# A U weights' cast placed behind a GELU, and gate one-hots built four tokens at a time, in a two-layer hybrid backbone

## The chip, the cores and the metric

The kernel runs on one core of a Trainium2 chip, in one launch. The metric is the time of an execution on the device in microseconds. Engines are named as in the profile: PE (TensorE, matmuls), PEld (its weight loads), DVE (VectorE), ACT (ScalarE), POOL (GpSimd) and SP (SyncE, which here only issues DMA transfers).

## The reference

Two layers work on 512 latent tokens and 256 context tokens of width 1024 in float32. In each layer a modulated norm feeds a token mixer (grouped-query attention and an RWKV-7 scan in two directions), and then a modulated norm feeds a layer of product-key experts (PEER):

```python
def peer_ffn(h, w_query, subkeys1, subkeys2, expert_u, expert_v):
    q = (h @ w_query).reshape(B, L, PEER_HEADS, 2, PEER_HALF)
    s1 = jnp.einsum('blhd,kd->blhk', q[..., 0, :], subkeys1)
    s2 = jnp.einsum('blhd,kd->blhk', q[..., 1, :], subkeys2)
    ...  # top 16 of each, top 16 of their sums: expert_idx; gates = softmax(top_score)
    u = jnp.take(expert_u, i_blk, axis=0)
    act = gelu(einsum('td,ted->te', h_blk, u))           # exact GELU
    v = jnp.take(expert_v, i_blk, axis=0)
    out = einsum('te,ted->td', g_blk * act, v)
```

There are 8 heads with 16 experts each for every token, out of 128 x 128 = 16384 experts. An expert's number is i1 * 128 + i2. The second layer needs no expert output for the context tokens.

## The kernel before

**Dense and gathered tokens.** Most token blocks (128 tokens each) go through *all* experts as dense products; the sparse choice enters as a weight that is zero for the experts that a token did not choose. In the first layer (`l == 0`) all four latent blocks are dense (`nd = 4`, 512 tokens, `TD = 512`) and the two context blocks are gathered, expert by expert, with indirect DMAs of GpSimd and multiply-adds of VectorE. In the second layer three latent blocks are dense and one is gathered. Gather steps are spread over the other work: `gafter(ins)` puts the next few of them behind an instruction `ins` of VectorE.

**A U product** (`ustep`) is the product of 128 experts' U rows (one value of i1) with all dense tokens, followed by the GELU. The weights come by a 512 KB DMA into a `raw` buffer. ScalarE casts them to `uhi` (`A.copy`, L1470), VectorE makes the remainder `ulo = ut - uhi` (L1471), and TensorE makes 24 matmuls (`mm3`, L158: 8 slices of the contraction, and for each high x high, high x low, low x high; the third is the first that reads `ulo`) into the PSUM tile `u_ps`. ScalarE's GELU (L1476) reads `u_ps` and writes `ga`. There are two `uhi` and two `ulo` buffers. The `raw` buffers (three in the first layer) are shared with the V weights (`vraw`).

**The gates' stretch.** For every dense block the chosen experts' i1, i2 and gates are transposed into `T3` (tile `gT`). `gstep` handles four tokens: it builds a one-hot of i2 times the gate (`o2`) and a one-hot of i1 (`o1`), both [128 choices, 128 places] for each token, and TensorE multiplies them (L1558) into `g_ps`: the 128 x 128 map of a token's gates. ScalarE copies it to `Gs` (L1560), from where it goes to DRAM (`gscr`). `o2` is made by four VectorE instructions, one a token (L1555: compare `iota` with i2, multiply by the gate). `o1` is made for odd groups by one VectorE comparison over four tokens (L1547), and for even groups by ScalarE: four Abs of `iota - i1` (L1552) and one Relu of one minus that (L1553). Each one-hot has three buffers. The first layer has 128 such steps, the second 96. Merged with them run U products whose `ga` is spilled to DRAM (`ustep(True)`): 43 in the first layer.

**The output stretch.** For each i1, `load_v` fetches and splits 128 V rows (`vhi` by ScalarE, `vlo` by VectorE), `load_u` fetches the spilled `ga` (as `gal`) or makes a new U product three steps ahead (`ustep(False)`, 85 in the first layer), and `weigh` multiplies `ga` by the gates `Gt` (a load of 1024 KB for every four i1) and splits the result into `whi` (ScalarE) and `wlo` (VectorE). `piece` then adds the products `whi`/`wlo` x `vhi`/`vlo` of two i1 (first layer) to the output: six of the eight pieces of the first layer gather in PSUM (`pa`), two go through one extra bank `po` and are added to SBUF by VectorE (L1637). PSUM is full in the first layer in this stretch: `u_ps` has *one* bank there (`ups[1] = 1`), and two in the second layer and in the gates' stretch.

**What sets the order.** The program names engine, operation and tiles. A planner (the Tile framework) turns it into one queue for each engine: it goes by the order of the program as priority, a model of each instruction's duration, and which buffer is free when. Each engine then works through its queue in that order and waits, at each instruction, for what that one needs. `merge` interleaves lists of steps in the program's order. `tc.issue_after(ins)` adds one more condition: the instructions in its block stand behind `ins` in the queue of its engine.

Of the kernel before, what the change touches and what calls it, by code (L numbers as in the profile page):

```python
# [10 lines left out]
F32 = mybir.dt.float32  # L11
# [5 lines left out]
AF = mybir.ActivationFunctionType  # L17
ALU = mybir.AluOpType
# [83 lines left out]
def body(ctx: ExitStack, tc: tile.TileContext, I: dict, out: bass.AP):  # L102
    nc = tc.nc
    V, A, G, PE, SP = nc.vector, nc.scalar, nc.gpsimd, nc.tensor, nc.sync
    mul, add, sub = ALU.mult, ALU.add, ALU.subtract
# [7 lines left out]
    def K(name):  # L113
        o, n = COFF[name]
        return cst[:, o:o + n]
# [38 lines left out]
    def mm3(ps, pairs, first, last):  # L154
        n = len(pairs)
        for q, (whi, wlo, hhi, hlo) in enumerate(pairs):
            for j, (a, b) in enumerate(((whi, hhi), (whi, hlo), (wlo, hhi))):
                PE.matmul(ps, a, b, start=first and q == 0 and j == 0, stop=last and q == n - 1 and j == 2)  # L158
# [1170 lines left out]
    def tail(L, cat, last, ro, need_ctx):  # L1329
        l = L["l"]  # L1330
# [40 lines left out]
        def gafter(ins, f=1.0):  # L1371
            pace[0] += pace[1] * f
            n = int(pace[0])
            pace[0] -= n
            if n and gq:
                with tc.issue_after(ins.ins):
                    gnext(n)
# [13 lines left out]
        op = eo.enter_context(tc.tile_pool(name=f"op{l}", bufs=1, side="right"))  # L1391
# [59 lines left out]
        pe = es.enter_context(tc.tile_pool(name=f"pe{l}", bufs=1))  # L1451
        gscr = dp.tile([NTC, 128, 128, GTC], F32, name=f"gscr{l}")
        gas = {}
        ucnt = [0]

        def raw():
            return pe.tile([128, KD, 128], F32, name="raw", bufs=RWB[l])
# [1 line left out]
        def wtiles():  # L1459
            return (raw(), pe.tile([128, KD, 128], F32R, name="uhi", bufs=2),  # L1460
                    pe.tile([128, KD, 128], F32R, name="ulo", bufs=2))

        def ustep(spill):
            i1 = ucnt[0]
            if i1 >= 128:
                return
            ucnt[0] += 1
            ut, uhi, ulo = wtiles()
            SP.dma_start(ut, I[f"ut{l}"][i1].rearrange("p (k c) -> p k c", c=128))
            A.copy(uhi, ut)  # L1470
            ins = V.tensor_tensor(ulo, ut, uhi.bitcast(F32), op=sub)  # L1471
            gafter(ins)
            ps = ups[0].tile([128, TD], F32, name="u_ps", bufs=ups[1])
            mm3(ps, [(uhi[:, k, :], ulo[:, k, :], hhi[:, k, :TD], hlo[:, k, :TD]) for k in range(KD)], True, True)
            ga = pe.tile([128, TD], F32, name="ga", bufs=5)
            A.activation(ga, ps, AF.Gelu)  # L1476
            if spill:
                gd = dp.tile([128, TD], F32, name=f"ga{l}_{i1}")
                SP.dma_start(gd, ga)
                gas[i1] = (gd, None)  # L1480
            else:
                gas[i1] = (None, ga)
# [18 lines left out]
        wp = e1.enter_context(tc.tile_pool(name=f"pt{l}", bufs=1, side="right"))  # L1501
# [35 lines left out]
        def gstep(q, b, t0):  # L1537
            T3 = R[b]["T3"]
            if t0 % GTC == 0:
                R["Gs"] = gsp.tile([128, 128, GTC], F32, name="Gs")  # L1540
            Gs = R["Gs"]
            gp = pp.tile([128, 4, 128], F32, name="g_ps", tag="q_ps", bufs=2)
            o1 = wp.tile([128, 4, 128], F32, name="oh1", bufs=3)
            o2 = wp.tile([128, 4, 128], F32, name="oh2", bufs=3)
            io = K("iota")
            if (t0 // 4) % 2:
                V.tensor_tensor(o1, io[:, None, :].to_broadcast([128, 4, 128]),  # L1547
                                T3[:, 0, t0:t0 + 4, None].to_broadcast([128, 4, 128]), op=ALU.is_equal)
            else:
                od = wp.tile([128, 4, 128], F32, name="ohd", bufs=2)  # L1550
                for t in range(4):
                    A.activation(od[:, t, :], io, AF.Abs, scale=-1.0, bias=T3[:, 0, t0 + t:t0 + t + 1])  # L1552
                A.activation(o1, od, AF.Relu, scale=-1.0, bias=1.0)  # L1553
            for t in range(4):
                V.tensor_scalar(o2[:, t, :], io, T3[:, 1, t0 + t:t0 + t + 1], T3[:, 2, t0 + t:t0 + t + 1],  # L1555
                                op0=ALU.is_equal, op1=mul)
            for t in range(4):
                PE.matmul(gp[:, t, :], o2[:, t, :], o1[:, t, :], start=True, stop=True)  # L1558
            tl = t0 % GTC
            A.copy(Gs[:, :, tl:tl + 4], gp.rearrange("p t i -> p i t"))  # L1560
            if tl + 4 == GTC:
                SP.dma_start(gscr[(128 * q + t0) // GTC], Gs)

        seq = []
        for q, b in enumerate(dn):
            if q == 0:
                seq += topk2(wp, wp, tk[b], R[b])
            if q == 0 and gl:
                for c in gl:
                    seq += topk2(wp, gr, tk[c], R[c]) + [lambda c=c: gather(c)]  # L1570
            nxt = topk2(wp, wp, tk[dn[q + 1]], R[dn[q + 1]]) if q + 1 < nd else []
            gs = [lambda b=b: gprep(b)] + [lambda q=q, b=b, t=t: gstep(q, b, t) for t in range(0, 128, 4)]
            k = len(gs) // (len(nxt) + 1)
            for i, f in enumerate(gs):
                seq.append(f)
                if nxt and i % k == k - 1:
                    seq.append(nxt.pop(0))
            seq += nxt
        merge((0.0, 1.0, seq), (0.0, 1.0, [lambda: ustep(True)] * nsp), (0.0, 1.0, [lambda: gnext(1)] * GP[l][1]))
        for _ in range(NTX[l]):  # L1580
            ustep(True)
        e2.close()
        e1.close()
        with tc.tile_pool(name=f"pv{l}", bufs=2, side="right") as pv, \
# [21 lines left out]
            def load_u(i1, r):  # L1606
                while i1 not in gas:
                    ustep(False)
                gd, ga = gas.pop(i1)
                if ga is None:  # L1610
                    ga = pe.tile([128, TD], F32, name="gal", tag="ga", bufs=5)
                    SP.dma_start(ga, gd)
                r["ga"] = ga
# [68 lines left out]
    for l in range(2):  # L1682
# [29 lines left out]
        last = rwkv(L, PT, cat, FD, need_ctx, ro, rl)  # L1712
        rl_es.close()
        tail(L, cat, last, ro_es, need_ctx)


# [64 lines left out]
```

## Time and profile before

| | us |
|---|---|
| median of 3 runs | 4747.82 (4742.24 to 4757.47) |
| the profiled execution | 4753.17 |
| its span | 4751.4 |
| PE busy in it | 4288.6 (90%) |
| DVE busy | 3619.3 (76%) |
| ACT busy | 1952.0 (41%) |
| POOL busy | 1366.7 (29%) |
| casts of U weights (L1470), both layers | 256, 1051 ns each |
| remainders of U weights (L1471) | 256, 1226 ns each |

The first layer's gates' stretch lies at about 1118 to 1488 us of the span, its output stretch at 1497 to 2757 us; the first product there that isn't spilled starts at 1717.9 us, the last at about 2730 us. The second layer's gates' stretch lies at about 3655 to 3925 us, its output stretch behind it. Busy time is the sum over a stretch of the time in which an engine has an instruction under way; a group's mean duration overlaps with its neighbours', so starts are compared where a price is wanted. A wait is the idle time of an engine in front of an instruction, put down to the instruction or the transfer that ended it.

### The profile page before, as it was taken

The numbers are of one execution on the slowest core, as the hardware profiler recorded it, in microseconds if no ns is written. First come the engines' busy times: TensorE is split into PE (matmuls) and PEld (weight loads), VectorE is DVE, ScalarE is ACT, GpSimd is POOL, SyncE is SP. The second block draws the span as 40 slices with busy tenths as digits, with TensorE's granted clock in tenths as the row PEclk, the third lists the DMA queues.
The fourth block names the chain that finished last, engine by engine and source line by source line (L and its number), as shares of the span: only waits on it lengthen the run. The fifth ranks groups of instructions, "written<-read, shape, count | busy, mean of one in ns | idle before, by whom it ended". The sixth has DMA issues, their size and how long they took to land. (4 is left out here: it accounts for less than half of the span.)

```text
span 4751.4 us, 85354 instructions
## 1 busy us (share of the span) xinstructions
PE 4288.6 (90%) x32715; PEld 3568.5 (75%) x32715; DVE 3619.3 (76%) x7842; ACT 1952.0 (41%) x3407; POOL 1366.7 (29%) x1256
## 2 busy tenths in 40 slices
PE   6998688877999999988899989868898999999999
PEld 4664576766787887767687778457678997899998
DVE  3457675899997888877788746766589967888885
ACT  3355343436674232222222234644336763333332
POOL 0201002442222345555455221200222102244441
PEclk8999898998999999999999999989899999999999
DMA  6656415435779999988898632651525769999995
GB/s 242 236 178 196 103 39 192 160 124 186 253 264 330 333 321 330 316 302 295 288 330 317 236 123 85 203 132 30 175 90 192 255 249 332 345 330 336 333 326 209
DMA packets 576904, 1106.71 MB, mean 233 GB/s; under 512 B 145328, under 2 KB 358000, under 8 KB 566768
## 3 DMA queue, kind: packets, MB, share of 16 engines
q1 hardware_dynamic: 465904, 698.56, 43.0%
q0 software_dynamic: 110592, 402.70, 23.6%
q8 instruction: 257, 4.21, 0.4%
q14 instruction: 151, 1.24, 0.1%
HBM read 960.37 MB, written 140.74 MB: 232 GB/s over the span
## 5 line engine op out<-in xcount | busy, mean ns | idle before, releaser
L158 PE MATMUL u_ps<-phi,uhi 128*128 128x512 f32 (+1 forms) x2048 | 765.1, 374 | 65.2 <-ACT ga L1476 48.4
L1285 POOL DMA_INDIRECT u<-in_u,eidx x384 | 485.7, 1265 | 1173.1 <-DVE u L1297 836.0
L158 PE MATMUL u_ps<-phi,ulo 128*128 128x512 f32 (+1 forms) x2048 | 757.3, 370 | 34.1 <-DVE ulo L1471 34.1
L158 PE MATMUL u_ps<-plo,uhi 128*128 128x512 f32 (+1 forms) x2048 | 753.3, 368 | 0.0
L1285 POOL DMA_INDIRECT u<-in_v,eidx x384 | 517.7, 1348 | 518.1 <-DVE gacc L1310 434.5
L1470 ACT CAST uhi<-raw 128x1024 fp32r<-128x1024 f32 x256 | 269.0, 1051 | 933.9 <-PE u_ps L158 546.6
L158 PE MATMUL pa<-vhi,whi 128*128 128x512 f32 x1536 | 601.5, 392 | 10.5 <-ACT whi L149 10.5
L158 PE MATMUL pa<-vlo,whi 128*128 128x512 f32 x1536 | 601.2, 391 | 0.0
L158 PE MATMUL pa<-vhi,wlo 128*128 128x512 f32 x1536 | 600.9, 391 | 0.0
L1297 DVE SCALAR_TENSOR_TENSOR u<-u,gh 128x1024 f32<-128x1024 f32 x384 | 468.3, 1230 | 120.2 <-DMA u<-in_u,eidx 112.4
L1310 DVE SCALAR_TENSOR_TENSOR gacc<-u,gw,gacc 128x1024 f32<-128x1024 f32 x381 | 488.4, 1282 | 93.3 <-DMA u<-in_v,eidx 89.8
L158 PEld LDWEIGHTS u_ps<-phi,uhi 128*128 128x128 f32 x2048 | 392.6, 192 | 120.2 <-ACT ga L1476 58.6
L158 PEld LDWEIGHTS u_ps<-phi,ulo 128*128 128x128 f32 x2048 | 391.3, 191 | 81.0 <-DVE ulo L1471 38.9
L158 PEld LDWEIGHTS u_ps<-plo,uhi 128*128 128x128 f32 x2048 | 392.2, 192 | 44.2
L1471 DVE TENSOR_TENSOR ulo<-raw,uhi 128x1024 fp32r<-128x1024 f32 x256 | 313.8, 1226 | 143.4 <-ACT uhi L1470 139.6
L149 ACT CAST whi<-w 128x512 fp32r<-128x512 f32 (+1 forms) x256 | 145.5, 568 | 601.3 <-DVE w L1618 384.0
L158 PEld LDWEIGHTS pa<-vhi,whi 128*128 128x128 f32 x1536 | 290.4, 189 | 69.8 <-issue 10.8
L158 PEld LDWEIGHTS pa<-vhi,wlo 128*128 128x128 f32 x1536 | 289.9, 189 | 61.4
L158 PEld LDWEIGHTS pa<-vlo,whi 128*128 128x128 f32 x1536 | 290.2, 189 | 58.7
L1604 DVE TENSOR_TENSOR vlo<-vraw,vhi 128x1024 fp32r<-128x1024 f32 x256 | 312.3, 1220 | 27.7 <-ACT vhi L1603 27.6
L1603 ACT CAST vhi<-vraw 128x1024 fp32r<-128x1024 f32 x256 | 263.7, 1049 | 66.4 <-PE pa L158 37.6
L1555 DVE TENSOR_SCALAR oh<-cst,gT 128x128 f32<-128x128 f32 x896 | 254.1, 362 | 0.6 <-ACT gT L1535 0.5
(867 smaller groups left out, 8603.8 us busy)
## 6 DMA issues: line engine op xcount, KB each, us to landing
raw<-in_ut SPq DMA_DIRECT2D x256, 512.0 KB
vraw<-in_v SPq DMA_DIRECT2D x256, 512.0 KB
gscr<-Gs SPq DMA_DIRECT2D x28, 2048.0 KB
mod_w<-in_mod_w SPq DMA_DIRECT2D x48, 1024.0 KB
Gt<-gscr SPq DMA_DIRECT2D x32, 1024.0 KB
raw<-in_w_q SPq DMA_DIRECT2D x48, 512.0 KB
Gt<-gscr SPq DMA_DIRECT2D x32, 768.0 KB
wo<-in_w_out SPq DMA_DIRECT2D x40, 512.0 KB
```

Of the source, the lines that this page charges most:

```text
L149: A.copy(hi, src)
L158: PE.matmul(ps, a, b, start=first and q == 0 and j == 0, stop=last and q == n - 1 and j == 2)
L1285: G.indirect_dma_start(out=t, out_offset=None, in_=I[f"{tab}{l}"], in_offset=bass.IndirectOffsetOnAxis(ap=res["e"][:, e:e + 1], axis=0))
L1297: V.scalar_tensor_tensor(u, u, 1.0, c["h"], op0=mul, op1=mul, accum_out=c["act"][:, e:e + 1])
L1310: V.scalar_tensor_tensor(acc, v, w[:, e:e + 1], acc, op0=mul, op1=add)
L1470: A.copy(uhi, ut)
L1471: ins = V.tensor_tensor(ulo, ut, uhi.bitcast(F32), op=sub)
L1555: V.tensor_scalar(o2[:, t, :], io, T3[:, 1, t0 + t:t0 + t + 1], T3[:, 2, t0 + t:t0 + t + 1], op0=ALU.is_equal, op1=mul)
L1603: A.copy(r["vhi"], vt)
L1604: gafter(V.tensor_tensor(r["vlo"], vt, r["vhi"].bitcast(F32), op=sub), f)
```

## The change

Two edits, both in `tail`. The first: `ulast` keeps the GELU instruction of the U product that was last written. In the first layer, for products that aren't spilled, the cast of the next product's weights gets the condition that it stands behind that GELU in ScalarE's queue. The second: in both layers, all one-hots are made by VectorE comparisons over four tokens at once, `o2` and `o1` alike, and the gate is multiplied in by ScalarE, one Copy with a scale by partition for each token, in place.

```diff
--- before.py
+++ after.py
@@ -1451,7 +1451,7 @@
         pe = es.enter_context(tc.tile_pool(name=f"pe{l}", bufs=1))
         gscr = dp.tile([NTC, 128, 128, GTC], F32, name=f"gscr{l}")
         gas = {}
-        ucnt = [0]
+        ucnt, ulast = [0], []
 
         def raw():
             return pe.tile([128, KD, 128], F32, name="raw", bufs=RWB[l])
@@ -1467,13 +1467,17 @@
             ucnt[0] += 1
             ut, uhi, ulo = wtiles()
             SP.dma_start(ut, I[f"ut{l}"][i1].rearrange("p (k c) -> p k c", c=128))
-            A.copy(uhi, ut)
+            if ulast and not spill and l == 0:
+                with tc.issue_after(ulast[0]):
+                    A.copy(uhi, ut)
+            else:
+                A.copy(uhi, ut)
             ins = V.tensor_tensor(ulo, ut, uhi.bitcast(F32), op=sub)
             gafter(ins)
             ps = ups[0].tile([128, TD], F32, name="u_ps", bufs=ups[1])
             mm3(ps, [(uhi[:, k, :], ulo[:, k, :], hhi[:, k, :TD], hlo[:, k, :TD]) for k in range(KD)], True, True)
             ga = pe.tile([128, TD], F32, name="ga", bufs=5)
-            A.activation(ga, ps, AF.Gelu)
+            ulast[:] = [A.activation(ga, ps, AF.Gelu).ins]
             if spill:
                 gd = dp.tile([128, TD], F32, name=f"ga{l}_{i1}")
                 SP.dma_start(gd, ga)
@@ -1542,18 +1546,11 @@
             gp = pp.tile([128, 4, 128], F32, name="g_ps", tag="q_ps", bufs=2)
             o1 = wp.tile([128, 4, 128], F32, name="oh1", bufs=3)
             o2 = wp.tile([128, 4, 128], F32, name="oh2", bufs=3)
-            io = K("iota")
-            if (t0 // 4) % 2:
-                V.tensor_tensor(o1, io[:, None, :].to_broadcast([128, 4, 128]),
-                                T3[:, 0, t0:t0 + 4, None].to_broadcast([128, 4, 128]), op=ALU.is_equal)
-            else:
-                od = wp.tile([128, 4, 128], F32, name="ohd", bufs=2)
-                for t in range(4):
-                    A.activation(od[:, t, :], io, AF.Abs, scale=-1.0, bias=T3[:, 0, t0 + t:t0 + t + 1])
-                A.activation(o1, od, AF.Relu, scale=-1.0, bias=1.0)
+            io = K("iota")[:, None, :].to_broadcast([128, 4, 128])
+            V.tensor_tensor(o2, io, T3[:, 1, t0:t0 + 4, None].to_broadcast([128, 4, 128]), op=ALU.is_equal)
+            V.tensor_tensor(o1, io, T3[:, 0, t0:t0 + 4, None].to_broadcast([128, 4, 128]), op=ALU.is_equal)
             for t in range(4):
-                V.tensor_scalar(o2[:, t, :], io, T3[:, 1, t0 + t:t0 + t + 1], T3[:, 2, t0 + t:t0 + t + 1],
-                                op0=ALU.is_equal, op1=mul)
+                A.activation(o2[:, t, :], o2[:, t, :], AF.Copy, scale=T3[:, 2, t0 + t:t0 + t + 1])
             for t in range(4):
                 PE.matmul(gp[:, t, :], o2[:, t, :], o1[:, t, :], start=True, stop=True)
             tl = t0 % GTC
```

## Rows read from the trace of the kernel before

**Rows 1.** Busy table by stretch: start:end, length, busy (count) by engine, clock, DMA, GB/s.

```profile
1118.00:1488.00 370.00, 348.06 (x1977) 298.48 (x1975) 350.41 (x982) 268.17 (x556) 81.81 (x75) 0.98 0.70 254
...
1717.00:1980.00 263.00, 253.48 (x1106) 206.70 (x1105) 226.08 (x223) 71.58 (x92) 142.60 (x105) 1.00 0.91 324
1980.00:2380.00 400.00, 352.08 (x1471) 283.63 (x1470) 301.62 (x432) 94.82 (x123) 199.16 (x147) 0.96 0.85 296
...
3655.00:3925.00 270.00, 263.17 (x1738) 260.52 (x1737) 230.39 (x576) 195.64 (x395) 29.65 (x27) 0.99 0.69 252
```

**Rows 2.** Waits of TensorE, 1717 to 2741 us: total us, times, longest.

```profile
PE u_ps L158 <- ACT ga L1476: 43.2, 19, 6.6
PE po L158 <- DVE acc L1637: 25.7, 9, 7.3
```

**Rows 3.** Waits of ScalarE, the same stretch.

```profile
ACT uhi L1470 <- PE u_ps L158: 235.4, 39, 8.0
ACT uhi L1470 <- DMA raw<-in_ut: 234.0, 34, 13.4
```

**Rows 4.** ScalarE in order of time: start, us, instruction, count, [idle before, releaser].

```profile
1838.76 1.05 ACT L1470 CAST uhi<-raw 128x1024 fp32r<-128x1024 f32 x1 [7.49 <-DMA raw<-in_ut]
1839.71 0.59 ACT L1476 ACTIVATE ga<-u_ps 128x512 f32<-128x512 f32 x1
1845.95 1.06 ACT L1470 CAST uhi<-raw 128x1024 fp32r<-128x1024 f32 x1 [5.64 <-PE u_ps L158]
...
1858.89 1.06 ACT L1470 CAST uhi<-raw 128x1024 fp32r<-128x1024 f32 x1 [5.14 <-DMA raw<-in_ut]
...
1867.84 1.06 ACT L1470 CAST uhi<-raw 128x1024 fp32r<-128x1024 f32 x1 [7.39 <-PE u_ps L158]
```

**Rows 5.** VectorE in order of time, the same round (subtractions of U weights).

```profile
1839.84 1.23 DVE L1471 TENSOR_TENSOR ulo<-raw,uhi 128x1024 fp32r<-128x1024 f32 x1
...
1850.55 1.22 DVE L1471 TENSOR_TENSOR ulo<-raw,uhi 128x1024 fp32r<-128x1024 f32 x1
...
1864.91 1.22 DVE L1471 TENSOR_TENSOR ulo<-raw,uhi 128x1024 fp32r<-128x1024 f32 x1
...
1872.27 1.22 DVE L1471 TENSOR_TENSOR ulo<-raw,uhi 128x1024 fp32r<-128x1024 f32 x1
```

**Rows 6.** TensorE in order of time: first matmul between products, first of each product.

```profile
1833.43 0.39 PE L158 MATMUL pa<-vhi,whi 128*128 128x512 f32 x1
...
1840.36 0.50 PE L158 MATMUL u_ps<-phi,uhi 128*128 128x512 f32 x1 [1.30 <-ACT ga L1476]
...
1852.77 0.39 PE L158 MATMUL u_ps<-phi,uhi 128*128 128x512 f32 x1
...
1862.36 0.39 PE L158 MATMUL u_ps<-phi,uhi 128*128 128x512 f32 x1
...
1873.30 0.39 PE L158 MATMUL u_ps<-phi,uhi 128*128 128x512 f32 x1
```

**Rows 7.** Groups by line, gates' stretch, first layer: count | busy us, mean ns.

```profile
L1552 ACT ACTIVATE ohd<-cst,gT 128x128 f32<-128x128 f32 x256 | 83.1, 398 | 0.4
...
L1553 ACT ACTIVATE oh<-ohd 128x512 f32<-128x512 f32 x64 | 40.6, 635 | 0.0
...
L1555 DVE TENSOR_SCALAR oh<-cst,gT 128x128 f32<-128x128 f32 x512 | 146.4, 368 | 0.5 <-ACT gT L1535 0.5
...
L1547 DVE TENSOR_TENSOR oh<-cst,gT 128x512 f32<-128x512 f32 x64 | 44.7, 699 | 0.7 <-PE g_ps L1558 0.7
```

**Rows 8.** VectorE in order of time, in the gates' stretch.

```profile
1455.49 0.70 DVE L1547 TENSOR_TENSOR oh<-cst,gT 128x512 f32<-128x512 f32 x1
1456.09 1.12 DVE L1555 TENSOR_SCALAR oh<-cst,gT 128x128 f32<-128x128 f32 x4
```

**Rows 9.** Waits of TensorE, 1118 to 1488 us.

```profile
PE g_ps L1558 <- DVE oh L1555: 9.9, 9, 1.6
PE u_ps L158 <- DVE ulo L1471: 4.6, 7, 1.1
```

## Prediction

> **What bounds the kernel now.** I read the busy table by stretch first, then TensorE's waits in the stretch, then ScalarE's, then the order of single instructions over one round. The table [rows 1] shows two kinds of stretch. In the gates' stretches of both layers (1118 to 1488 us and 3655 to 3925 us) TensorE is busy 348.1 of 370 us and 263.2 of 270 us; VectorE is busy 350.4 of 370 us in the first. In the first layer's output stretch, once the U products run in it (1717 to about 2741 us), TensorE is busy 253.5 of 263 us before 1980 us, but 352.1 of 400 us behind it, with a granted clock of 0.96 in the mean: a small part at the lower of its two levels (1.2 against 2.4 GHz), in a stretch in which it has idled. A matmul costs 253.48/1106 = 0.229 us in the full-clock part and 352.08/1471 = 0.239 us in the other: 1471 x 0.010 = 15 us lie in the clock. What TensorE waits for there [rows 2] is the GELU, 43.2 us in 19 waits, and the vector add that frees the extra bank, 25.7 us in 9. Why the GELU is late stands in [rows 3]: ScalarE's cast of U weights waited 234.0 us in 34 places for its own weights and 235.4 us in 39 for TensorE. ScalarE takes its queue in order, and in that queue the cast stands directly ahead of the GELU [rows 4].
>
> **Which cast that is.** There are two `uhi` buffers, so the cast that starts when product k's matmuls run out (1840.36 + 24 x 0.229 = 1845.9 against 1845.95 us [rows 4, 6]) needs the buffer that k read, and is that of product k+2. The vector subtraction of k+1 was made in the round before [rows 5]: weights are ready a whole product ahead. The first layer has one `u_ps` bank here, so product k+1 cannot start before GELU k has read it. The order is: product k ends, cast k+2, GELU k, product k+1. When the weights of k+2 are late, GELU k is late, and TensorE stops when its other matmuls (`pa`, `po`) between the products are used up: in [rows 6] the product at 1840.36 us starts 0.06 us after the GELU ended (1839.71 + 0.59) [rows 4], after 1.30 us of waiting.
>
> **The change, output stretch.** `ulast` holds the GELU of the last U product that was written before, so cast k+1 is put behind GELU k: not k+2, which is the one that stands in the way, but one nearer. Cast k+2 then lies behind GELU k+1. This removes the stop of GELU k by late weights of k+2. It adds a chain between two products: product k ends, GELU k 0.59 us, cast k+1 1.05 us, subtraction k+1 1.22 us on VectorE, product k+1. The second buffers of `uhi` and `ulo` stay without use. Behind the cast in ScalarE's queue stand the casts of V weights and of the weighed gates, as now.
>
> The chain by numbers. Instructions of ScalarE overlap by 0.10 us (1838.76 + 1.05 against 1839.71 [rows 4]), and a hand-over to the next engine takes 0.06 us (GELU to product, above), so the cast ends 0.06 + 0.59 + 0.95 = 1.6 us after product k. With d the time from the cast's end to the subtraction's end, and the third matmul of a product as the first that reads `ulo` (two spacings of 0.23 us later), product k+1 starts 1.6 + d + 0.06 - 0.46 = 1.2 + d after product k. The least d is the subtraction alone: 1839.84 + 1.23 against the cast's end at 1839.81, 1.26 us [rows 4, 5]. In the other three of the round, the subtraction ends at 1851.77, 1866.13 and 1873.49 us, its cast at 1847.01, 1859.95 and 1868.90: d is 4.8, 6.2 and 4.6 us, since VectorE works off its own queue (226.1 of 263 us busy [rows 1]).
>
> What covers it: the matmuls between two products. Products start at 1840.36, 1852.77, 1862.36 and 1873.30 us [rows 6]; less 24 x 0.229 = 5.5 us of product, the gaps are 6.9, 4.1 and 5.4 us, and the gap that began at 1833.43 us had 5.5 us of work and 1.3 us of waiting. The rounds repeat every four products (one load of gates); 85 products (128 less 43 spilled) are 21 rounds.
>
> Upper end: VectorE keeps the order of now. The four products of the round then start 1.2 + d after the one before: the first only when the late weights are in (the cast starts at 1838.76 us, 5.3 us after the product; 5.3 + 1.05 + 1.26 + 0.06 - 0.46 = 7.2), then 6.0, 7.4 and 5.8 us. Less the cover of 5.5, 6.9, 4.1 and 5.4 us: 1.7 + 0 + 3.3 + 0.4 = 5.4 us a round, 1.3 of it there now: 4.1 x 21 = +86 us. Lower end: weights always in time, the subtraction at once; 1.2 + 1.26 = 2.5 us is covered everywhere, the 43.2 us of GELU waits go, and the 15 us of clock with them: -58 us. Middle: the order is written by a planner that sees the new chain and will set the subtraction earlier, so that d halves towards its least (1.26, 3.0, 3.7, 2.9): 1.7 + 0 + 0.8 + 0 = 2.5 us a round, +1.2 x 21 = +25 us. I take +45, between the last and the upper end: the nearest rows are those of VectorE's queue, which at 86% busy can't let the subtraction pass much, and idle time takes clock as it does behind 1980 us.
>
> Why the late weights don't become early: loads of U and V weights share three buffers, and a buffer comes free when its subtraction is done. Casts keep their place in time (now at a product's end, then a GELU later); only the number of the product that they serve moves. So loads start and land as now, with one product less in store.
>
> **The change, gates.** For a pair of token groups VectorE now makes 8 comparisons of 128 columns (146.4/512 = 0.286 us each) and one of 512 (44.7/64 = 0.70 us; 0.60 from one start to the next) [rows 7, 8]: 2.9 to 3.0 us. Then it makes four of 512: 2.4 to 2.8 us. That is 0.1 to 0.6 us less, over 64 pairs 6 to 38 us of VectorE in the first layer. ScalarE makes four Abs (83.1/256 = 0.325 us) and one Relu (40.6/64 = 0.63 us) a pair, 1.93 us; then eight multiplies with a scale by partition, taken as Abs with a bias by partition: 2.6 us. That is 0.67 us more, 43 us in the first layer (268.2 becomes 311 of 370 us) and 32 us for the 48 pairs of the second (195.6 becomes 228 of 270 us [rows 1]). The multiplies now stand between VectorE and TensorE, in the queue in which the cast waits for a product's end. What TensorE waits for from VectorE here is 9.9 + 4.6 = 14.5 us [rows 9]: that is all there is to gain in the first layer. At worst, with one group of four multiplies (1.3 us) uncovered behind each of 43 products, +56 us; three buffers of each one-hot are the cover. I take -5 us, near the wait row, and nothing in the second layer, where TensorE is busy 97%. The Trainium skill (ScalarE: Activation LUTs, "Rules for kernel authors") says to use VectorE, not ScalarE, for a multiply, which speaks against this half; the rows have VectorE at 95% and ScalarE at 72% of the stretch, so I let the rows decide. The Trainium skill (VectorE: DVE Perf Modes, "Mode 2x_2P") says that an fp32 operation with one tensor source runs at two elements a cycle and one with two sources at one; by that alone the four-token form would stream 512 elements in 0.53 us against 0.27 us, a loss of 0.27 us a group (my estimate, +34 us of VectorE in the first layer); the rows show 0.60 to 0.70 against 4 x 0.286 = 1.14 us, so the count of instructions weighs more.
>
> **Sum.** The profiled execution took 4753.2 us, 5.4 above the median of 4747.8. 4753.2 + 45 - 5 = 4793, as a median 4788 us.
>
> **Rivals.** (A) The GELU is freed and nothing follows: it decides if the weights of k+1 are in when GELU k ends, in nearly every round, and VectorE subtracts at once. For it: 235.4 us of the casts' waits are for TensorE, with weights already there, and one product more of patience is all that the 34 late ones lack. Against: loads share three buffers and start no earlier, and the 25.7 us for the extra bank stay. Of 58 us I give it two thirds: -35 - 5, median 4708, the faster side. Chance 0.25. (B) A wash: the planner spreads the `pa` matmuls so that each gap covers the chain, and new waits take the place of the old: +25 less what the GELU gives back, within 15 us of 4745. Chance 0.2. (C) The output stretch as in B, but ScalarE, in order and at 84%, becomes late for the gates: half of the 56 us, 4775. For it: casts that wait there hold up the multiplies; against: the three buffers. Chance 0.07. The Trainium skill's rule on multiplies, named above (ScalarE: Activation LUTs, "Rules for kernel authors"), speaks for this one. That the edit doesn't bind can be excluded: in [rows 4] each cast stands ahead of the GELU of two products before. The forecast, slower by the chain, has 0.48, with a range of its own of 4765 to 4870.
>
> What can be told from no change is 0.3%, 14 us. Faster: A 0.25, and 0.10 from B and the forecast's low tail: 0.35. Same: 0.15, mostly B. Slower: 0.50. The range 4700 to 4870 takes in A and the upper end without the worst of the gates.
>
> **What would show it.** Right: each U cast behind the GELU of the product just before it; TensorE's GELU waits nearly gone, and in their place waits for `uhi` or `ulo` of over 80 us in the output stretch; the stretch from the first unspilled product to the last 30 to 90 us longer; casts still waiting for `raw` loads; VectorE's gates share down by 6 to 38 us and ScalarE's up by some 40. Wrong: subtractions that end under 2 us behind their casts, gaps between products of 5 us or more throughout, or a stretch under 1000 us, which is A.

## The result, and the profile after

The changed kernel took 4774.18 us (median of 5 runs, 4766.42 to 4774.49) against 4747.82 us (median of 5, 4742.24 to 4760.98): ratio 1.0052 [1.0038, 1.0066], 26 us slower. Its profiled execution is the shortest of its five, 4766.42 us, 13.2 us above that of the kernel before, so the two traces show only a part of the medians' distance.

The stretch from the first U product that isn't spilled to the last has 4058 matmuls in both kernels. The busy table by stretch, first the row of before for exactly this piece (start:end, length, busy of PE, PEld, DVE, ACT, POOL, clock, DMA share, GB/s):

```profile
1717.90:2735.70 1017.80, 948.90 (x4058) 770.44 (x4057) 809.33 (x932) 261.89 (x338) 500.60 (x370) 0.98 0.85 301
```

The same table of after, with the gates' stretches of both layers, and 400 us inside the output stretch:

```profile
1113.00:1480.00 367.00, 350.95 (x1977) 296.46 (x1975) 337.19 (x666) 309.47 (x748) 94.25 (x75) 1.00 0.71 258
1705.00:2752.00 1047.00, 965.11 (x4058) 777.25 (x4057) 806.96 (x931) 263.04 (x339) 490.40 (x369) 0.97 0.84 293
1967.00:2367.00 400.00, 337.05 (x1355) 268.81 (x1354) 278.37 (x401) 87.68 (x114) 180.61 (x136) 0.92 0.80 275
3671.00:3940.00 269.00, 261.70 (x1726) 258.66 (x1725) 217.85 (x362) 222.63 (x527) 30.35 (x26) 0.99 0.68 250
```

The piece begins 12.9 us earlier (1705.0 against 1717.9), lasts 29.2 us longer (1047.0 against 1017.8), and what follows it takes 3.1 us less: -12.9 + 29.2 - 3.1 = +13.2 us, the distance of the spans. Of the 29.2 us, 13.0 are idle time of TensorE (81.9 against 68.9) and 16.2 are busy time of the same matmuls (965.1 against 948.9): the granted clock is 0.92 in the 400 us, against 0.96 in [rows 1], and a matmul costs 337.05/1355 = 0.249 us, against 0.239.

What TensorE waits for in after in that piece, to be read against [rows 2] (total us, times, longest):

```profile
PE u_ps L158 <- DVE ulo L1475: 71.9, 33, 5.8
PE u_ps L158 <- ACT uhi L1472: 9.9, 6, 3.8
```

Both waits of before are gone, that for the extra bank too, and 81.8 us of waits for weights stand in their place. The order in ScalarE's queue is as the edit asks (start, us, instruction, [idle before, releaser]):

```profile
2433.34 0.60 ACT L1480 ACTIVATE ga<-u_ps 128x512 f32<-128x512 f32 x1 [7.03 <-PE u_ps L158]
2433.83 1.04 ACT L1472 CAST uhi<-raw 128x1024 fp32r<-128x1024 f32 x1
...
2442.91 1.05 ACT L1600 CAST vhi<-vraw 128x1024 fp32r<-128x1024 f32 x1 [6.16 <-DMA vraw<-in_v]
2444.28 0.60 ACT L1480 ACTIVATE ga<-u_ps 128x512 f32<-128x512 f32 x1 [0.32 <-PE u_ps L158]
2444.78 1.04 ACT L1472 CAST uhi<-raw 128x1024 fp32r<-128x1024 f32 x1
```

One of the long stops of after, PE, DVE and ACT in order of time (what VectorE did before the late subtraction is the point):

```profile
2212.00 1.04 ACT L1472 CAST uhi<-raw 128x1024 fp32r<-128x1024 f32 x1
...
2214.78 1.23 DVE L1297 SCALAR_TENSOR_TENSOR u<-u,gh 128x1024 f32<-128x1024 f32 x1 [4.36 <-DMA u<-in_u,eidx]
...
2215.66 0.39 PE L158 MATMUL u_ps<-plo,uhi 128*128 128x512 f32 x1
...
2216.54 1.22 DVE L1601 TENSOR_TENSOR vlo<-vraw,vhi 128x1024 fp32r<-128x1024 f32 x1
2217.67 1.22 DVE L1297 SCALAR_TENSOR_TENSOR u<-u,gh 128x1024 f32<-128x1024 f32 x1
...
2219.42 1.22 DVE L1297 SCALAR_TENSOR_TENSOR u<-u,gh 128x1024 f32<-128x1024 f32 x1
...
2220.57 1.22 DVE L1475 TENSOR_TENSOR ulo<-raw,uhi 128x1024 fp32r<-128x1024 f32 x1
...
2221.84 0.79 PE L158 MATMUL u_ps<-phi,ulo 128*128 128x512 f32 x1 [5.80 <-DVE ulo L1475]
...
2222.43 0.63 PE L158 MATMUL u_ps<-phi,uhi 128*128 128x512 f32 x1
```

The cast ended at 2213.04 us. VectorE had stopped for 4.36 us at a gather step whose row had not landed, and then worked off what stood ahead of the subtraction, which came 7.5 us after the cast. TensorE had made the two matmuls that need no `ulo` and stopped for 5.80 us. Its next matmuls start 0.43 us apart instead of 0.23, until 2227.6 us: the granted clock of that stretch is 0.51, the lower of the two levels. This is the common case: 13 of the stops at `ulo` are longer than 1.6 us and make up 54 of the 72 us, and in each of them VectorE had stood still for a row (12 of them) or for `vhi` (the other), at a time between 4 us ahead of the cast's start and the subtraction.

So VectorE's own waits are the next view, before and then after:

```profile
DVE u L1297 <- DMA u<-in_u,eidx: 83.4, 40, 10.1
DVE gacc L1310 <- DMA u<-in_v,eidx: 81.2, 72, 4.1
DVE ulo L1471 <- ACT uhi L1470: 16.3, 8, 4.8
```

```profile
DVE u L1297 <- DMA u<-in_u,eidx: 97.3, 40, 5.4
DVE gacc L1310 <- DMA u<-in_v,eidx: 64.9, 38, 5.5
DVE ulo L1475 <- ACT uhi L1472: 29.4, 15, 8.5
DVE vlo L1601 <- ACT vhi L1600: 25.4, 17, 3.2
```

VectorE has little slack. Its account of before is 809.3 busy, 164.6 waiting for gathered rows, 26.2 for casts (16.3 above and 9.9 for `whi`), and 17.7 of anything else: 1017.8 us. That of after is 807.0, 162.2, 60.3 (29.4, 25.4, 5.5) and 17.5: 1047.0 us. The 29.2 us are 34.1 us more of waits for ScalarE's casts, of `uhi` and of `vhi`, less 4.9 us in the other three. Why `vhi` is late stands in ScalarE's waits of after, against [rows 3], where 234.0 us went to `raw` loads of U weights and V loads didn't stand out (5.2 us in 3):

```profile
ACT vhi L1600 <- DMA vraw<-in_v: 261.7, 41, 12.0
```

The late loads have moved from U weights to V weights. From the issue of its load to the end of its subtraction, a U weight holds one of the three shared buffers for 15.0 us before and 23.1 us after (medians over the piece), and a V weight for about 22 and 15 us. What SyncE's queue waits for shows the link: V loads wait there for the subtraction of a U weight, which frees a buffer. Before and then after:

```profile
SPq L1600 <- DVE ulo L1471: 192.1, 41, 9.2
```

```profile
SPq L1597 <- DVE ulo L1475: 359.8, 40, 12.7
```

U loads wait for the same subtractions 270.8 us before and 102.4 after; the sum of the two kinds stays at 462 to 463 us.

### The profile page after: what moved, and what is told of

The parts are those of the page before. It is cut to its first block, busy times and chain, and to the rows that moved or that the text cites. A ratio compares the mean times of both kernels' runs of the same rounds, so it can differ in the third digit from the quotient of the medians.

```text
span 4764.6 us, 85220 instructions
## 1 busy us (share of the span) xinstructions
PE 4302.4 (90%) x32715; PEld 3570.9 (75%) x32715; DVE 3590.5 (75%) x7282; ACT 2020.2 (42%) x3743; POOL 1365.4 (29%) x1256
## 3 DMA queue, kind: packets, MB, share of 16 engines
q1 hardware_dynamic: 465904, 698.56, 43.2%
## 5 line engine op out<-in xcount | busy, mean ns | idle before, releaser
L158 PE MATMUL u_ps<-phi,ulo 128*128 128x512 f32 (+1 forms) x2048 | 768.9, 375 | 100.4 <-DVE ulo L1475 100.1
L158 PE MATMUL u_ps<-phi,uhi 128*128 128x512 f32 (+1 forms) x2048 | 769.6, 376 | 33.3 <-ACT uhi L1474 17.7
L1285 POOL DMA_INDIRECT u<-in_v,eidx x384 | 506.3, 1318 | 528.9 <-DVE gacc L1310 452.9
L158 PEld LDWEIGHTS pa<-vhi,whi 128*128 128x128 f32 x1536 | 289.1, 188 | 68.9 <-issue 10.5
L1474 ACT CAST uhi<-raw 128x1024 fp32r<-128x1024 f32 x171 | 179.0, 1048 | 340.8 <-PE u_ps L158 185.7
L1553 ACT ACTIVATE oh<-oh,gT 128x128 f32<-128x128 f32 x896 | 288.5, 397 | 31.9 <-DVE oh L1550 29.2
```

The lines of the kernel that those rows point to most:

```text
L1285: G.indirect_dma_start(out=t, out_offset=None, in_=I[f"{tab}{l}"], in_offset=bass.IndirectOffsetOnAxis(ap=res["e"][:, e:e + 1], axis=0))
L1553: A.activation(o2[:, t, :], o2[:, t, :], AF.Copy, scale=T3[:, 2, t0 + t:t0 + t + 1])
```

## The experiments

**First round: which half, and is it the nearness of the cast?** Theory 1: the loss is the chain GELU, cast, subtraction in one product's time. Rival (theory 2): transfers bind, and the order only chooses where TensorE waits. Cast condition alone:

```diff
-            A.copy(uhi, ut)
+            if ulast and not spill and l == 0:
+                with tc.issue_after(ulast[-1]):
+                    A.copy(uhi, ut)
...
-            A.activation(ga, ps, AF.Gelu)
+            ulast.append(A.activation(ga, ps, AF.Gelu).ins)
```

> The cast's condition alone (first layer's output stretch), gates' one-hots as before. Theory 1 (the chain GELU, cast, subtraction now lies between two products, and VectorE's queue is the long part of it): all of the loss is in this half, and the gates give some 10 us back, so this is slower than the changed kernel too: +20 to +40 us against before, ratio 1.004 to 1.008, with 60 to 90 us of TensorE waits for the subtraction and next to none for the GELU. Rival (the loss comes from the gates, or from transfers that the new order shifts in both halves): within 12 us of before.

Measured: 4774.15 us, 1.0056 [1.0043, 1.0068]: as long as the changed kernel's 4774.18, where the expectation had it slower. The loss is all in this half. In the piece, the instructions of VectorE and ScalarE come in the same order as in the changed kernel. The gates alone:

```diff
...
-                V.tensor_scalar(o2[:, t, :], io, ..., op0=ALU.is_equal, op1=mul)
+            V.tensor_tensor(o2, io, T3[:, 1, t0:t0 + 4, None]..., op=ALU.is_equal)
+            V.tensor_tensor(o1, io, T3[:, 0, t0:t0 + 4, None]..., op=ALU.is_equal)
+                A.activation(o2[:, t, :], o2[:, t, :], AF.Copy, scale=T3[:, 2, t0 + t:t0 + t + 1])
```

> The one-hots by four-token comparisons alone, the cast free as before. Theory 1: -5 to -15 us against before (0.997 to 0.999), since the first layer's last gate product comes 8 us earlier in the changed kernel's trace; the output stretch as before, with 35 to 50 us of TensorE waits for the GELU. Rival (the multiplies on ScalarE cost what VectorE saves): within 5 us of before or slower.

Measured: 4743.71 us, 0.9996 [0.9987, 1.0005]; theory 1's 5 to 15 us were not there, the rival's bound held. The order in the piece is that of the kernel before. If nearness were the cause, a condition one GELU further back should cure it: cast k behind GELU k-2, with the new gates and with the old.

```diff
-            if ulast and not spill and l == 0:
-                with tc.issue_after(ulast[0]):
+            if len(ulast) > 1 and not spill and l == 0:
+                with tc.issue_after(ulast[-2]):
                     A.copy(uhi, ut)
...
-            ulast[:] = [A.activation(ga, ps, AF.Gelu).ins]
+            ulast.append(A.activation(ga, ps, AF.Gelu).ins)
```

> The changed kernel with one thing altered: the cast of product k's weights stands behind the GELU of product k-2, not k-1. Theory 1: the GELU is still never held up by a cast that waits for its load, and the subtraction is a whole product early again, so both the waits for the GELU (43 us before) and those for the subtraction (72 us in the changed kernel) fall under 20 us: 20 to 50 us faster than before (0.990 to 0.996). Rival 2 (the stretch is bound by the transfers, and each order only names another instruction as the one that waits): within 10 us of the gates alone.

> The cast of product k behind the GELU of product k-2, gates' one-hots as before. Theory 1: 15 to 45 us faster than before (0.991 to 0.997), GELU waits of TensorE in the output stretch from 43 us to under 15. Rival 2 (bound by transfers): within 10 us of before, the waits only under other names.

Measured: 4771.41 us, 1.0049 [1.0036, 1.0062], and 4779.77 us, 1.0064 [1.0049, 1.0079]. The cure failed. TensorE's waits in the first of the two:

```profile
PE po L158 <- DVE acc L1634: 80.0, 41, 5.2
PE u_ps L158 <- ACT ga L1480: 5.6, 5, 1.6
```

The GELU and the subtraction are nearly free now (5.6 and 1.1 us), as theory 1 wanted, and TensorE stops at the extra bank instead, whose add stands in VectorE's queue. Three orders of the cast, three places of the stop, and VectorE's queue stands behind each: at the add and the subtraction directly, at the GELU by the loads that wait for its subtractions. Theory 1 as the whole cause falls. The rival's bound was missed as well: 28 us above the gates alone and 33 above the kernel before, where it allowed 10.

**Second round: is it VectorE's stop at late rows?** Theory 3: VectorE, in order, stops at gather steps whose rows have not landed, and TensorE waits at whatever stands behind them; the cast's order chooses the place. If so, without the gather transfers the two orders cost the same. The transfers of the first layer's output stretch are left out, before and after; VectorE's steps stay and read a resident tile (the first layer's expert output of the context tokens is not computed).

```diff
+            if nodma[0]:
+                return t
...
-            V.scalar_tensor_tensor(u, u, 1.0, c["h"], ...)
+            V.scalar_tensor_tensor(u, c["h"] if nodma[0] else u, 1.0, c["h"], ...)
...
-            v, w, acc = row("v", e), c["w"], c["acc"]
+            v, w, acc = c["h"] if nodma[0] else row("v", e), c["w"], c["acc"]
...
+            nodma[0] = l == 0
```

> The kernel before, with the gather transfers of the first layer's output stretch left out: VectorE's gather steps stay, of the same length, but read a tile that is already there, so none of them waits (the context tokens' expert output of the first layer is not computed). Theory 3 (what the runs so far point to: VectorE's queue stops at gather steps that wait for their rows, some 160 us in each version, and TensorE's idle time is whatever instruction stands behind them, the add for the extra bank, the cast ahead of the GELU through late loads, or the subtraction): TensorE's waits for the GELU and for the add fall from 69 us to under 20, and with the clock the run is 50 to 90 us faster than before. Theory 1 (only the chain of the instructions themselves counts): the GELU waits stay at 30 to 45 us, less than 30 us faster.

> The changed kernel with the same left out. Theory 3: TensorE's waits for the subtraction fall from 72 us to under 20, and this run lies within 10 us of the kernel before with the gather transfers left out: the changed order costs only where VectorE stops. Theory 1: VectorE is still busy and the subtraction still waits for its turn; 20 to 40 us slower than that kernel, with over 50 us of waits for the subtraction.

Measured: 4648.41 us, 0.9795 [0.9781, 0.9808], and 4642.40 us, 0.9777 [0.9764, 0.9790]: 96 us faster than before, somewhat more than theory 3's 50 to 90, and 6 us from each other, where it allowed 10. The busy table of the same 4058 matmuls, order of before, then of after:

```profile
1707.90:2633.10 925.20, 925.20 (x4058) 761.50 (x4057) 808.76 (x930) 258.52 (x338) 0.00 (x0) 1.00 0.39 121
```

```profile
1706.80:2631.90 925.10, 925.10 (x4058) 761.42 (x4057) 801.18 (x929) 263.97 (x338) 0.00 (x0) 1.00 0.38 122
```

TensorE never stops, the granted clock is 1.00, and VectorE has 116 to 124 us of room. The new chain is covered in full: the order costs nothing where VectorE has that room. V loads are late in the new order even here (ScalarE's wait and SyncE's):

```profile
ACT vhi L1605 <- DMA vraw<-in_v: 124.4, 41, 5.5
```

```profile
SPq L1602 <- DVE ulo L1479: 368.8, 42, 12.7
```

With the order of before, ScalarE waits for no load at all in this experiment. So it is the order that makes V weights late, with gather traffic or without it; VectorE waits 1.3 us for them here, and 25.4 us in the real kernel. In the real kernel, waits and clock together take 1017.8 - 925.2 = 92.6 us in the order of before and 121.9 in that of after. This run takes away the waits for rows and a part of the traffic at once (121 instead of 301 GB/s), so it doesn't tell these two apart. Nor is VectorE's queue quite the same: the planner places the instructions anew, and 64 of VectorE's 810 in the piece are out of the order that they had (56 of 812 with the new order; 13 and 4 of ScalarE's 338).

Two repairs in the same round. The subtraction with an earlier due time for the planner:

```diff
-            ins = V.tensor_tensor(ulo, ut, uhi.bitcast(F32), op=sub)
+            with late(-2000 if l == 0 and not spill else 0):
+                ins = V.tensor_tensor(ulo, ut, uhi.bitcast(F32), op=sub)
```

> The changed kernel, with the subtraction of the U weights given an earlier priority in the planner (first layer, products that aren't spilled), so that VectorE takes it before other work that is ready. Theory 1: the time from the cast's end to the subtraction's end falls from 3.5 us in the mean towards 1.3 to 2, the waits for it from 72 us to under 35, 15 to 35 us faster than the changed kernel, that is within 10 us of before. Theory 3: the planner takes gather rows as in time where they aren't, so gather steps that wait still stand ahead of the subtraction; within 12 us of the changed kernel.

Measured: 4765.19 us, 1.0046 [1.0033, 1.0060]. Waits for `ulo` are 67.6 us in 31 against 71.9 in 33. But the edit hardly acted: only 3 of VectorE's 812 instructions in the piece change their order, and from the cast's end to the subtraction's it takes 3.5 us in the mean, as against 3.4. Whether a better place in the queue would help is not shown by it. And, on the version with the farther cast, the extra bank read out by ScalarE, so that VectorE no longer holds it:

```diff
+                elif l == 0:
+                    pt = pv.tile([128, 512], F32, name="pt", bufs=1)
+                    A.copy(pt, po)
+                    V.tensor_tensor(acc[q][:, hs_], pt, acc[q][:, hs_], op=add)
```

> The cast behind the GELU of two products before (as in the third run), and the extra bank copied out by ScalarE, so that VectorE adds from there and TensorE no longer waits for VectorE's queue at all. Theory 3: the 80 us of waits for the add fall under 25 us, and nothing takes their place: 30 to 60 us faster than before. Rival 2 (transfers: ScalarE's queue then stops at casts whose loads are late, 130 us of such waits in the third run): the waits for the extra bank stay above 50 us under ScalarE's name, and the run lies within 15 us of the third run.

Measured: 4796.81 us, 1.0108 [1.0093, 1.0124], 25 us slower than without it. TensorE's waits, and ScalarE in order of time at the second longest stop (6.8 us, until 1990.07):

```profile
PE po L158 <- ACT pt L1635: 64.7, 16, 7.3
PE u_ps L158 <- ACT ga L1480: 22.9, 6, 4.9
```

```profile
1988.48 1.04 ACT L1600 CAST vhi<-vraw 128x1024 fp32r<-128x1024 f32 x1 [13.98 <-DMA vraw<-in_v]
1989.43 0.58 ACT L1635 COPY pt<-po 128x512 f32<-128x512 f32 x1
```

In all 16 stops at `po` the copy starts as soon as the instruction ahead of it in ScalarE's queue is done, and VectorE's last add from `pt` had ended 7 to 15 us earlier. So the one `pt` isn't the cause. What stands ahead is the cast of V weights in 11 of the 16, 10 of them after a wait of 10 to 14 us for its load. That is the rival's way (64.7 us under ScalarE's name, over 50), though not its size (25 us, where it allowed 15).

**Third round: rows earlier, with all transfers in place.** GpSimd issues a row only when VectorE has freed one of four buffers (its waits, before):

```profile
POOL u L1285 <- DVE gacc L1310: 233.7, 165, 5.0
POOL u L1285 <- DVE u L1297: 162.9, 77, 13.7
```

Two more buffers in the output stretch lengthen the lead and leave every transfer in. Theory 3a: the stops go because rows are asked for sooner. Theory 3b: transfers bind, and more lead brings nothing.

```diff
-            t = gr.tile([128, D], F32, name="u", bufs=UB[l])
+            extra[1] = (extra[1] + 1) % 6
+            if extra[0] is not None and extra[1] < 2:
+                t = extra[0].tile([128, D], F32, name="ux", bufs=2)
+            else:
+                t = gr.tile([128, D], F32, name="u", bufs=UB[l])
...
+            extra[0] = pv if l == 0 else None
```

> The kernel before with six buffers for gathered rows in place of four in the first layer's output stretch; all transfers and all VectorE work stay. Theory 3a (a row's transfer can start only when VectorE has freed a buffer, so with four buffers every delay of VectorE comes back as a late row, and TensorE's idle time is that): VectorE's waits for rows fall from 165 us to under 90, TensorE's waits for the GELU and the add from 69 us to under 40, 20 to 60 us faster than before. Theory 3b (the transfers themselves are the limit: the 16 DMA engines are 85% busy and a row takes as long as the traffic lets it): VectorE's waits stay above 120 us, within 15 us of before.

Measured: 4680.26 us, 0.9857 [0.9837, 0.9876], 68 us faster (20 to 60 expected). Busy table, TensorE's waits and VectorE's waits for rows:

```profile
1709.30:2664.60 955.30, 933.67 (x4058) 764.28 (x4057) 811.54 (x933) 259.49 (x339) 497.29 (x368) 0.99 0.90 320
```

```profile
PE u_ps L158 <- ACT ga L1482: 16.9, 8, 5.0
PE po L158 <- DVE acc L1644: 4.6, 3, 1.9
```

```profile
DVE u L1303 <- DMA u<-in_u,eidx: 33.8, 15, 4.1
DVE ux L1303 <- DMA ux<-in_u,eidx: 24.1, 10, 7.9
```

Waits for rows fall from 164.6 to 59 us, TensorE's from 68.9 to 21.5, and the rate rises to 320 GB/s: 301 was no ceiling ([rows 1] has 324 in the first 263 us). 3a holds. With the buffers the planner also moved 41 of VectorE's 810 instructions; what that does by itself was not tried. The same buffers under the changed order:

> The changed kernel with six row buffers. Theory 3a: the waits for the subtraction fall from 72 us to under 40 and this run comes within 12 us of the kernel before with six buffers. Theory 3b: as slow as the changed kernel within 15 us, 15 to 35 us slower than the kernel before with six buffers.

Measured: 4714.30 us, 0.9931 [0.9914, 0.9948]. The expectation (within 12 us of the run above) fell: 34 us are left. TensorE's, ScalarE's and VectorE's waits:

```profile
PE u_ps L158 <- DVE ulo L1481: 40.5, 19, 8.4
```

```profile
ACT vhi L1607 <- DMA vraw<-in_v: 248.1, 41, 14.1
```

```profile
DVE vlo L1608 <- ACT vhi L1607: 56.7, 30, 3.9
DVE ulo L1481 <- ACT uhi L1478: 47.0, 26, 7.7
```

VectorE waits as little for rows as in the run above (62 us), but 109 us for casts, where the old order has 67.5 (48.5 for `uhi`, 19.0 for `whi`, none for `vhi`). So rows are not the only thing that stops its queue: a V weight that lands late does it too, and the changed order makes V weights late. The far cast and the gates alone, each with six buffers:

> The cast behind the GELU of two products before (and the new gates), with six row buffers. Theory 3a: the waits for the add fall from 80 us to under 45; no slower than the kernel before with six buffers by more than 10 us. Theory 3b: within 15 us of the same order with four buffers, which was 25 us slower than before.

> The gates' half of the change alone with six row buffers, the cast free as before. Theory 3a: the best of all, 20 to 60 us faster than before. Theory 3b: within 10 us of the gates' half alone, which was 3 us faster than before.

Measured: 4717.65 us, 0.9934 [0.9919, 0.9949], and 4677.94 us, 0.9851 [0.9834, 0.9867]. The far cast is no better than the near one here either: the waits for the add fell as expected (80.0 to 19.9 us), but it is 37 us slower than the old order, where 10 were allowed. VectorE waits 78.7 us for `vhi` in it. The last is the fastest version found, faster than both kernels; the new gates add nothing to it that can be told from the old (0.9857).

## Why the prediction came out as it did

The direction and the kind of cause were right; 26 us were measured where +40 was forecast (4788 against 4748).

- **Which cast, and what replaces the GELU waits: right.** The cast stands behind the GELU of the product just before it; the GELU waits are gone, and 81.8 us of `ulo` and `uhi` waits stand there ("over 80"). Two other signs were missed: the stretch grew by 29.2 us ("30 to 90"), and no cast of U weights waits for its load any more.
- **The output stretch's size: too large, +45 taken, +29.2 measured.** Read as waits alone, the 45 us were 72 us of new waits less the GELU's 1.3 us a round (27 us in 21 rounds), with no term for the extra bank. The new waits were sized well: 81.8 us. The measured d, from the cast's end to the subtraction's, has a mean of 3.4 us, between the 4.2 of the round's four values and the 2.7 of the halved ones; over the whole piece of before it is 5.3. What failed is what is given back: the GELU's whole 43.2 us of [rows 2], not 27, and the 25.7 us for the extra bank, which the text let stay. Once TensorE stops at `ulo`, the add that frees the bank, behind the same head of the queue, is done by the time it is asked for (argued from the order, not tried by itself). So 81.8 + 0.1 (other idle time) - 68.9 = +13.0 us of idle time, and 16.2 us that had no term of their own, the clock. That the total came within 16 us of +45 is partly luck: the new waits were 10 us more, what was given back was 42 us more, and the 16 us of clock fill part of the hole.
- **The clock: right in direction, and more than half of the loss.** 16.2 of the 29.2 us are busy time of the same matmuls, at a mean clock of 0.97 instead of 0.98. The text named it as a reason to go above the middle case, and didn't size it.
- **"Loads start and land as now": wrong.** U weights sit one product longer in buffers that V weights share; V loads come late instead of U loads. "Casts still waiting for `raw` loads" should have read: casts of V weights. By VectorE's account, in which the waits for rows are as long after as before, the growth is in the casts: 25.4 us for `vhi` and 13.1 us more for `uhi`.
- **What the prediction didn't see: VectorE's stops for rows.** It took VectorE's busy share (86% in [rows 1]) for what makes it late. Of the piece's 1017.8 us VectorE is idle for 208.5, and 164.6 of these are stops at rows with work queued behind.
- **The gates: right.** VectorE's busy time fell from 350.4 to 337.2 us, 191.1 to 175.4 in the one-hots (-16; forecast -6 to -38), ScalarE's is 309.5 us of the stretch (forecast 311) and 222.6 in the second layer (forecast 228). The groups by line of after, against [rows 7]; then TensorE's waits for them, one of before that [rows 9] doesn't have, and those of after:

```profile
L1553 ACT ACTIVATE oh<-oh,gT 128x128 f32<-128x128 f32 x512 | 164.0, 395 | 10.2 <-DVE oh L1550 7.9 <-DVE u L1297 1.1 <-DVE ttv L1209 1.0
...
L1550 DVE TENSOR_TENSOR oh<-cst,gT 128x512 f32<-128x512 f32 x128 | 87.8, 686 | 5.4 <-PE g_ps L1555 5.0
L1551 DVE TENSOR_TENSOR oh<-cst,gT 128x512 f32<-128x512 f32 x128 | 87.6, 684 | 0.0
```

```profile
PE g_ps L1558 <- ACT oh L1553: 3.2, 4, 1.2
```

```profile
PE g_ps L1555 <- ACT oh L1553: 8.0, 15, 1.3
PE g_ps L1555 <- DVE oh L1551: 2.0, 2, 1.2
```

  The waits for one-hots moved to ScalarE and shrank a little, from 13.1 to 10.0 us. For the time, -5 us was taken. The gates alone gave -3 (not told from none), and the first unspilled product starts at 1713.0 us in the mean over the five profiles with the old gates here (1707.9 to 1719.9) and at 1707.5 over the nine with the new (1702.8 to 1716.4), 5.5 us earlier. The 12.9 us between the first two traces are mostly scatter. The Trainium skill's rule to multiply on VectorE (ScalarE: Activation LUTs, "Rules for kernel authors") didn't decide here: 0.9996 with 512 such multiplies on ScalarE in this layer.
- **Rivals.** B's half of it came: new waits in the place of the old, with 13.0 us of idle time more; the clock took the time out of its 15 us. A's premise was met by the far cast, where the GELU is nearly free (5.6 us), and the stop went to the extra bank: no gain. C's time, 4775 us, is the one measured, but not its way: TensorE's waits for the gates fell. (A's two thirds of 58 us are 39, not 35; nothing hangs on it.)

Shown: the loss is in the cast's half; without the gather transfers the new order costs nothing; more lead for rows gives 68 us to the old order; the new order makes V loads wait for U weights' buffers, with the gather transfers and without them. Argued from VectorE's and ScalarE's waits, not tested alone: how much of the 29 us the late V weights cost. A fourth weight buffer would tell; it was not tried. Open: why the far cast is slower than before. Its VectorE waits 31 us longer for rows with four buffers, and 40 us longer for casts with six. Its casts of V weights wait 198.8 us for loads too, in 25 places, though a U weight holds its buffer there for 16.3 us, little longer than before, and V loads wait 188.3 us for the subtractions of U weights, no longer than before: the shared buffers don't explain that.

## What to carry to other kernels

When an engine that takes its queue in order feeds the bottleneck, read its *waits* beside its busy share: here each reorder of the consumers moved the stop from one name to another (GELU, extra bank, `ulo`) and left its cause. Look for what stops the head of that queue, and lengthen that transfer's lead: two more buffers were worth more than any order that was tried. And where two streams share a pool of buffers, holding one stream's buffer longer can make the *other* stream late (here V loads' waits for U weights' buffers went from 192 to 360 us). The Trainium skill (Perfetto Trace Analysis, "Optimization Strategy") says that gaps that come again and again can mean too little memory for the next tile; here four instead of six row buffers were that, 68 us.

## What was not expected of the hardware

- The clock's cost goes with TensorE's idle time, at 0.34 to 0.58 us for each us: 23.7 us of longer busy time (948.9 - 925.2) with 68.9 us idle in before, 39.9 with 81.9 in after, 8.5 with 21.6 in the old order with six buffers, 24.9 with 42.7 in the far cast with six, none with none (mean granted clock 0.98, 0.97, 0.99, 0.98 and 1.00).
- Four one-hots by one comparison of 512 columns take 0.686 us of VectorE, where one of 128, with the gate multiplied in, took 0.286: four of those are 1.14 us, so the count of instructions weighs more here than the columns. Multiplies of 128 columns on ScalarE have a duration of 395 ns, and 164.0/512 = 0.320 us each in a row.
